# A hybrid encoder layer on one core: seven block products instead of eight for the left half of the second feed-forward matrix in blocks 1 to 3, placed between row blocks of the first matrix

## The chip, the core and the metric

The kernel runs on one core of one Trainium2 chip. Its time is the device time of that core in microseconds (us), from the first to the last instruction. Before the change it is 1097.86 us, the median of 3 runs (1096.95 to 1099.26). Engines are named as in the profile: PE (matmuls), PEld (weight loads of PE), DVE (vector engine), ACT (scalar engine), POOL (GpSimd) and SP (the queue that issues most loads).

## The reference, cut to what matters

One layer: a windowed attention sub-layer, then a feed-forward sub-layer, each with a modulation by the vector c ahead of it and a LayerNorm behind it. The change touches the feed-forward part alone.

```python
D_MODEL, SEQ, D_FF = 2048, 256, 8192
def sq_relu_mlp(h, w1, b1, w2, b2):
    u = jnp.square(jax.nn.relu(h @ w1 + b1))      # (256, 8192)
    return u @ w2 + b2                            # (256, 2048)

mod = c_act @ mod_w[i] + mod_b[i]
sh_m, sc_m, g_m, sh_f, sc_f, g_f = jnp.split(mod, 6, axis=-1)
...
hmlp = x * (1.0 + sc_f) + sh_f
y = sq_relu_mlp(hmlp, mlp_w1[i], mlp_b1[i], mlp_w2[i], mlp_b2[i])
x = layer_norm(DEEPNORM_ALPHA * x + (1.0 + g_f) * y, ln_mlp_g[i], ln_mlp_b[i])
```

All of it is float32.

## The kernel before

A float32 product is made of three matmuls on rounded operands: each operand is split into a high part (a cast) and a low part (the rest), and high by high, high by low and low by high are summed in PSUM. `mm3` (L497 to L500) issues the three; its 128 x 512 output takes three matmuls of 512 columns.

**The weight stream.** `Stream` holds a queue of pieces of weights, each 128 x 2048 in float32 (1 MB), in the order in which the program uses them. `loads` (L196) issues them from SP into the buffers of the pool `raws` (5 in this stage); ACT casts each half of a piece to a `wh` tile of 128 x 1024 (L247), DVE subtracts that from the piece to make the `wl` tile (L218), and there are 5 buffers for either kind. `main` hands the next piece to the matmuls, and `done` says that PE has finished with half a piece. Some pieces are not for matmuls: 16 pieces `in_modgf` make the feed-forward gate, each two DVE instructions of 1024 columns (L345).

**The feed-forward part.** The 8192 hidden units are worked in 4 blocks of 2048. Block 0's first matrix (L971 to L973) is built another way and isn't touched. For blocks 1 to 3 `ff_hidden` makes 16 row blocks of 128 hidden units: 16 times a matmul of 512 columns (L995, weights high; the right side is the input's high and low part side by side, 256 each) and one of 256 columns (L996, weights low) into one PSUM bank. `square_halves` then adds the two halves of the bank (ACT L943, DVE L944), squares what is above zero (DVE L946), and splits it (ACT L948, DVE L949) into `u`, two row blocks to a tile. `ff_out` multiplies all 2048 hidden units of the block by 512 columns of the second matrix, for 4 column groups c and 2 row halves t of the sequence: 96 matmuls of 512 columns for each c. Their result is added to `ys` by DVE; in the last block `add_gated` applies the gate, adds the input and takes the statistics.

So in each block a stage of row blocks (L995, L996) is followed by a stage of output (L498 to L500). A tile scheduler sets the order on each engine from the program's order and the buffers that come free; each engine then runs its own queue strictly in that order. PSUM has 8 banks: pool `psa` with 5 (names pa), `pst` with 2 (pt), `psm` with 1 (pm).

Of the kernel before, what the change touches and what calls it, by code (L numbers as in the profile page):

```python
# [20 lines left out]
S = 256  # L21
# [27 lines left out]
def hybrid_kernel(ctx: ExitStack, tc: tile.TileContext, a, out: bass.AP):  # L49
# [55 lines left out]

    def masks():
        msk = cst.tile([128, NT, 256], F32, name="msk")
# [8 lines left out]
    def rotary_tables():  # L116
# [17 lines left out]
        trig = cst.tile([128, 2, 3, NT, 32], F32, name="trig")  # L134
# [39 lines left out]
    class Stream:  # L174
# [4 lines left out]
        def __init__(self):  # L179
# [11 lines left out]
            self.side = {}  # L191

        def plan(self, src, use=None, kept=0):
            self.q.append((src, use, kept))

# [9 lines left out]
        def freed(self, n):  # L205
            if self.deep or self.home[n] is raws:
                self.free.append(self.home[n])
# [6 lines left out]
        def low(self):  # L214
            n = len(self.ls)
            r, kept = self.src[n]
            l = (g4, g4b)[kept - 1](F32R) if kept else wlp.tile([128, 1024], F32R, name="wl")
            self.pinned(nc.vector.tensor_sub(l, r, f32(self.hs[n])))  # L218
            self.ls.append(l)
            if n % 2:  # L220
                self.freed(self.of[n])

        def pump(self, vecs, must=0):

            while len(self.ls) < must or self.at < len(self.q):
# [17 lines left out]
                if n >= must and (n - self.used >= self.nh or kept):  # L243
                    return
                h = (g4, g4b)[kept - 1](F32R) if kept else whp.tile([128, 1024], F32R, name="wh")
                s = self.raw[self.at][:, n % 2 * 1024:n % 2 * 1024 + 1024]
                self.pinned(nc.scalar.copy(h, s))  # L247
                self.hs.append(h)
                self.src.append((s, kept))
                self.of.append(self.at)  # L250
                self.at += n % 2

        def main(self):
            i = self.im
            self.pump(self.pace, 2 * i + 2)
            self.im += 1
            h, l = self.hs[2 * i:2 * i + 2], self.ls[2 * i:2 * i + 2]
# [219 lines left out]
    for blk in range(BLK):  # L477
        for f in range(NF):
            if blk:
                if blk == 1 and f % 2:  # L480
                    if f == 1:
                        first_gf = len(S.q)
                    m_gf.plan()
                S.plan(a["w1b"][(blk - 1) * NF + f])
        for c in range(4):
            for kg in range(4):
                if blk == 1 and kg % 2:
                    m_gf.plan()
                S.plan(a["w2"][blk, c, kg], None, max(kg - 1, 0) if blk == BLK - 1 and c == 3 else 0)
# [401 lines left out]
    S.stop = 0  # L891
# [48 lines left out]
    def square_halves(ps, ft, u, at):  # L940
# [235 lines left out]
```

## Time and profile before

| what | us |
|---|---|
| median of 3 runs | 1097.86 |
| span of the profiled execution | 1098.2 |
| PE busy | 1067.6 |
| DVE busy | 804.2 |
| ACT busy | 522.0 |
| POOL busy | 30.0 |

The page lists, among other things, busy time for each engine, the chain of work that ended last, and groups of instructions by line with their mean duration. The views drawn on below are the windows (busy time of each engine in a stretch), the timeline (single instructions in order of time), the groups of instructions with shapes kept apart, and the list of transfers. A matmul's duration in these views holds its way through the array and overlaps the next one, so what one costs is the distance between two starts.

### The profile page before, as it was taken

The numbers are of one execution on the slowest core, as the hardware profiler recorded it, in microseconds if no ns is written. First come the engines' busy times: TensorE is split into PE (matmuls) and PEld (weight loads), VectorE is DVE, ScalarE is ACT, GpSimd is POOL, SyncE is SP. The second block draws the span as 40 slices with busy tenths as digits, with TensorE's granted clock in tenths as the row PEclk, the third lists the DMA queues.
The fourth block names the chain that finished last, engine by engine and source line by source line (L and its number), as shares of the span: only waits on it lengthen the run. The fifth ranks groups of instructions, "written<-read, shape, count | busy, mean of one in ns | idle before, by whom it ended". The sixth has DMA issues, their size and how long they took to land.

```text
span 1098.2 us, 15487 instructions
## 1 busy us (share of the span) xinstructions
PE 1067.6 (97%) x6098; PEld 863.1 (79%) x6098; DVE 804.2 (73%) x1162; ACT 522.0 (48%) x806; POOL 30.0 (3%) x54
## 2 busy tenths in 40 slices
PE   8889999998999999999999999999999999999995
PEld 6657677665677799988888888888888888888884
DVE  4597899978899877754588889756666557665676
ACT  5333346765673537643344543344453334544340
POOL 1000000001000000000000010001000000000001
PEclk9989999999999999999999999999999999999998
DMA  9999987789985996555578788866555555557511
GB/s 384 425 427 425 427 357 280 271 297 379 377 315 201 361 360 244 185 192 192 195 301 303 272 313 306 312 220 225 184 189 190 197 196 186 178 185 267 191 75 77
DMA packets 43337, 292.70 MB, mean 267 GB/s; under 512 B 5104, under 2 KB 5232, under 8 KB 9472
## 3 DMA queue, kind: packets, MB, share of 16 engines
q1 hardware_dynamic: 39312, 279.85, 66.9%
q0 software_dynamic: 3200, 10.50, 2.7%
q10 hardware_dynamic: 752, 1.35, 0.3%
q8 instruction: 48, 0.79, 0.3%
q14 instruction: 25, 0.20, 0.0%
HBM read 289.57 MB, written 2.11 MB: 266 GB/s over the span
## 4 chain that ended last, share of the span: by engine, by line
PE 86%; DVE 7%; DMA 4%; ACT 2%; issue 1%; DVEq 0%; ACTq 0%
PE pa L995 16%; PE pa L500 15%; PE pa L498 15%; PE pa L499 15%; PE pa L996 8%; PE pa L972 3%; PE pa L971 3%; PE pa L973 3%; PE pm L307 3%; DVE wl L218 2%; DMA raw<-in_modm 2%; DMA raw<-in_modf 1%; DVE g L345 1%; DMA raw<-in_wqkv 1%; PE pa L687 1%; PE pa L743 1%
## 5 line engine op out<-in xcount | busy, mean ns | idle before, releaser
L218 DVE TENSOR_TENSOR wl<-raw,wh 128x1024 fp32r<-128x1024 f32 x332 | 403.9, 1223 | 223.6 <-ACT wh L247 222.9
L247 ACT CAST wh<-raw 128x1024 fp32r<-128x1024 f32 x332 | 347.1, 1051 | 441.3 <-PE pa L500 228.6
L498 PE MATMUL pa<-wh,g 128*128 128x512 f32 x816 | 324.1, 398 | 5.1 <-ACT g L519 2.6
L500 PE MATMUL pa<-wh,g 128*128 128x512 f32 x816 | 318.9, 392 | 4.1 <-DVE g L521 3.0
L499 PE MATMUL pa<-wl,g 128*128 128x512 f32 x816 | 320.0, 392 | 0.0
L995 PE MATMUL pa<-g,wh 128*128 128x512 f32 x768 | 270.1, 397 | 0.0
L996 PE MATMUL pa<-g,wl 128*128 128x256 f32 x768 | 214.9, 280 | 0.0
L498 PEld LDWEIGHTS pa<-wh,g 128*128 128x128 f32 x816 | 153.9, 189 | 46.8 <-issue 7.5
L500 PEld LDWEIGHTS pa<-wh,g 128*128 128x128 f32 x816 | 153.5, 188 | 41.2 <-DVE g L521 6.0
L499 PEld LDWEIGHTS pa<-wl,g 128*128 128x128 f32 x816 | 153.9, 189 | 33.0 <-issue 2.4
L995 PEld LDWEIGHTS pa<-g,wh 128*128 128x128 f32 x768 | 144.2, 188 | 36.0 <-issue 0.8
L996 PEld LDWEIGHTS pa<-g,wl 128*128 128x128 f32 x768 | 144.8, 189 | 0.1
L345 DVE SCALAR_TENSOR_TENSOR g<-raw,cact,g 128x1024 f32<-128x1024 f32 x65 | 82.6, 1280 | 2.8 <-DMA raw<-in_modf 2.3
L972 PE MATMUL pa<-g,wh 128*128 128x256 f32 x256 | 72.7, 285 | 0.4 <-DVE g L915 0.4
L971 PE MATMUL pa<-g,wh 128*128 128x256 f32 x256 | 72.5, 286 | 0.0
L973 PE MATMUL pa<-g,wl 128*128 128x256 f32 x256 | 72.3, 283 | 0.0
L307 PE MATMUL pm<-raw,cact 128*32 128x256 f32 (+2 forms) x776 | 48.8, 375 | 5.9 <-DMA raw<-in_modf 3.2
L971 PEld LDWEIGHTS pa<-g,wh 128*128 128x128 f32 x256 | 48.8, 192 | 1.3 <-issue 0.8
L972 PEld LDWEIGHTS pa<-g,wh 128*128 128x128 f32 x256 | 49.1, 192 | 0.9 <-DVE g L915 0.8
L973 PEld LDWEIGHTS pa<-g,wl 128*128 128x128 f32 x256 | 49.1, 192 | 0.0
L345 DVE SCALAR_TENSOR_TENSOR g4b<-raw,cact,g4b 128x1024 f32<-128x1024 f32 x32 | 40.7, 1280 | 9.0 <-DMA raw<-in_modgf 8.8
L307 PEld LDWEIGHTS pm<-raw,cact 128*32 128x32 f32 x776 | 20.9, 112 | 25.9 <-issue 11.5
(165 smaller groups left out, 741.6 us busy)
## 6 DMA issues: line engine op xcount, KB each, us to landing
raw<-in_w SPq DMA_DIRECT2D x64, 1024.0 KB, 4.9
raw<-in_w1b SPq DMA_DIRECT2D x48, 1024.0 KB, 5.0
raw<-in_modm SPq DMA_DIRECT2D x32, 1024.0 KB, 14.8
raw<-in_modf SPq DMA_DIRECT2D x32, 1024.0 KB, 6.9
raw<-in_wqkv SPq DMA_DIRECT2D x24, 1024.0 KB, 12.8
raw<-in_modgm SPq DMA_DIRECT2D x16, 1024.0 KB, 7.5
raw<-in_wo SPq DMA_DIRECT2D x16, 1024.0 KB, 7.5
raw<-in_w1a SPq DMA_DIRECT2D x16, 1024.0 KB, 7.6
```

What stands on the lines that cost most here:

```text
L218: self.pinned(nc.vector.tensor_sub(l, r, f32(self.hs[n])))
L247: self.pinned(nc.scalar.copy(h, s))
L307: i = nc.tensor.matmul(self.ps[32 * j:32 * j + 32, :w], lhsT[j] if type(lhsT) is list else lhsT, rhs[j], start=self.first, stop=stop)
L345: nc.vector.scalar_tensor_tensor(p[:, :e], s, cact[:, kt:kt + 1], p[:, :e], op0=OP.mult, op1=OP.add)
L498: nc.tensor.matmul(ps, xh, wh, start=start, stop=False)
L499: nc.tensor.matmul(ps, xh, wl, start=False, stop=False)
L500: S.prev = nc.tensor.matmul(ps, xl, wh, start=False, stop=stop).ins
L971: nc.tensor.matmul(o, wh(w, 128), hh, start=new, stop=False)
L972: nc.tensor.matmul(o, wh(w, 128), hl, start=False, stop=False)
L973: nc.tensor.matmul(o, wl(w, 128), hh, start=False, stop=end)
L995: nc.tensor.matmul(ps, wh(k, 128), hb, start=k == 0, stop=False)
L996: nc.tensor.matmul(ps[:, :256], wl(k, 128), hb[:, :256], start=False, stop=k == NK - 1)
```

## The change

**The products.** Take two row blocks of hidden units (k = 0, 1; a pair), the two sequence halves (t = 0, 1), and the column groups c = 0 and 1. That is a product of a 2 x 2 by a 2 x 2 matrix of blocks, eight block products before. Now there are seven, each over sums and differences of blocks (a Strassen-Winograd form), summed over the 8 pairs of a block in seven PSUM banks `pm[1]` to `pm[7]`. The sums of the hidden values are made by `sides` on DVE (tile `sc`), those of the weights by `sums` on DVE, in place in the loaded piece; at the block's end `gather` adds the seven banks to the four parts of `ys`. The right half (c = 2, 3) goes through `ff_out` as before.

**The order.** `ff_mixed` replaces `ff_hidden`. After row blocks 0 and 1 and 2, each pair i gives the products 1, 2, 3, then row block 2i+3, then the products 5, 7, 6, 4, then row block 2i+4. In a row block 8 matmuls of 512 columns now stand ahead of 8 of 256. With four `psa` banks taken by products, one is left for row blocks.

**The stream.** A piece for the products (`in_w2s`, 24 of them) makes four high and four low tiles (one of 512 columns, three of 1024); the last two pairs of tiles live in buffers of `raws`, of which 2 of the 5 are set aside (`reserve`).

**Moved.** The 16 gate pieces now lie between the pieces of block 0's output (14), and one each in blocks 1 and 2 (before: block 1). The bias b2 is loaded by quarters; the rescaling of the input goes to blocks 1 and 2, the gating of the finished parts (`base`) into block 3's stage. The square is taken on ACT (`square_half`) instead of DVE. Two small constant tables share the buffer of `sc`.

```diff
@@ Stream
+        def sums(self, raw, j):
+            while len(self.ls) < len(self.hs) - 1 and j > 1:
+                self.low()
+            if j == 2:
+                nc.vector.tensor_sub(raw[:, :1024], raw[:, 512:1536], raw[:, :1024])
+            if j == 3:
+                nc.vector.tensor_sub(raw[:, 1024:1536], raw[:, 1024:1536], raw[:, :512])
+                nc.vector.tensor_sub(raw[:, 1536:], raw[:, 1536:], raw[:, 1024:1536])
+            if j < 2:
+                return whp.tile([128, 1024], F32R, name="wh"), raw[:, :512] if j == 0 else raw[:, 1024:], None
+            x = raws.tile([128, 2048], F32R, name="raw")
+            return x[:, :1024], raw[:, 1024 * j - 2048:1024 * j - 1024], x[:, 1024:]
...
+    gf_fill = [1, 1, 1, 1, 1, 1, 1, 1, 1, 1, 1, 1, 1, 1, 0, 0, 1, 0, 0, 0, 0, 0, 0, 0, 1, 0, 0, 0, 0, 0, 0, 0]
...
+    for blk in range(1, BLK):
+        w1 = [a["w1b"][(blk - 1) * NF + f] for f in range(NF)]
+        S.plan(w1[0])
+        S.plan(w1[1])
+        for i in range(NP):
+            if i + 1 < NP:
+                S.plan(w1[2 * i + 2])
+            S.plan(a["w2s"][blk - 1, i], None, -1)
+            if i + 1 < NP:
+                S.plan(w1[2 * i + 3])
+        for c in (2, 3):
+            plan_out(blk, c)
...
-    def square_halves(ps, ft, u, at):
+    def square_half(ps, ft, u, uf, at):
         v = sml.tile([128, 512], F32, name="rl", tag="t2", bufs=4)
         nc.scalar.activation(v[:, 256:], ps[:, 256:], AF.Identity, bias=b1[:, ft:ft + 1])
         nc.vector.tensor_add(v[:, :256], v[:, 256:], ps[:, :256])
-        uf = sml.tile([128, 512], F32, name="uf", tag="t2", bufs=4)[:, :256]
-        nc.vector.scalar_tensor_tensor(uf, v[:, :256], 0.0, v[:, :256], op0=OP.max, op1=OP.mult)
+        nc.scalar.activation(v[:, 256:], v[:, :256], AF.Relu)
+        w = uf[:, at:at + 256]
+        nc.scalar.activation(w, v[:, 256:], AF.Square)
         h, l = u[:, at:at + 256], u[:, 512 + at:512 + at + 256]
-        nc.scalar.copy(h, uf)
-        nc.vector.tensor_sub(l, uf, f32(h))
+        nc.scalar.copy(h, w)
+        nc.vector.tensor_sub(l, w, f32(h))
+    def sides(uf):
...
+        nc.vector.tensor_add(q(0), p(1), p(3))
+        nc.vector.tensor_sub(q(1), q(0), p(0))
+        nc.vector.tensor_sub(q(2), p(0), p(1))
+        nc.vector.tensor_sub(q(3), p(2), q(1))
+        nc.scalar.copy(sc[:, :512], sf)
+        nc.vector.tensor_sub(sc[:, 512:], sf, f32(sc[:, :512]))
+        return sc
...
+            for k0 in (0, 8):
+                for k in range(k0, k0 + 8):
+                    nc.tensor.matmul(ps, wh(k, 128), ff_in(k), start=k == 0, stop=False)
+                for k in range(k0, k0 + 8):
+                    nc.tensor.matmul(ps[:, :256], wl(k, 128), ff_in(k)[:, :256], start=False, stop=k == NK - 1)
+                S.done()
...
+            product(1, i, u, 0, h[0], l[0], 0)
+            S.done()
+            product(2, i, u, 2, h[1], l[1], 1)
+            product(3, i, sc, 3, h[1], l[1], 0)
+            S.done()
+            yield
+            product(5, i, sc, 0, h[2], l[2], 0)
+            product(7, i, sc, 2, h[2], l[2], 1)
+            S.done()
+            product(6, i, sc, 1, h[3], l[3], 0)
+            product(4, i, u, 3, h[3], l[3], 1)
+            S.done()
+        hidden(0)
+        hidden(1)
+        sc = sides(pairs[0])
+        for i in range(NP):
+            g = chunk(i)
+            if i + 1 < NP:
+                hidden(2 * i + 2)
+            next(g)
+            if i + 1 < NP:
+                hidden(2 * i + 3)
+            for _ in g:
+                pass
+            if i + 1 < NP:
+                sc = sides(pairs[i + 1])
+            if i and more:
+                more.pop(0)()
+        return us, pm
+    def gather(pm):
...
+        return [add(y[0], y[0], pm[2]), lambda: nc.scalar.copy(w, pm[6]), add(y[1], y[1], pm[3]),
+                add(y[2], y[2], pm[4]), add(y[0], y[0], pm[1]), add(w, w, pm[1]), add(y[1], y[1], w),
+                add(y[1], y[1], pm[5]), add(y[3], y[3], pm[5]), add(w, w, pm[7]), add(y[2], y[2], w),
+                add(y[3], y[3], w)]
```

The next rows are the queues as built, with what each instruction waits for; lines are those of each version's own code.

PE, in the middle of a block, at the row block that stands between products 3 and 5 of a pair; `pt` and `pa` are PSUM banks, `sc` the tile of hidden sums, `raw` a buffer that holds weight sums. Before, in the row blocks:

```order
L995 MATMUL pa<-g_3389,wh 128x512 [waits Activation_49]
L996 MATMUL pa<-g_3389,wl 128x256 [waits DVE_49]
L995 MATMUL pa<-g_3389,wh 128x512
L996 MATMUL pa<-g_3389,wl 128x256
L995 MATMUL pa<-g_3390,wh 128x512
```

Now:

```order
L545 MATMUL pa<-wl,sc 128x512
L546 MATMUL pa<-wh,sc 128x512 [waits DVE_49]
L544 MATMUL pt<-raw,sc 128x512
L1060 MATMUL pa<-g_3388,wh 128x512 [waits DVE_49]
L1060 MATMUL pa<-g_3388,wh 128x512
L1060 MATMUL pa<-g_3389,wh 128x512 x2
L1060 MATMUL pa<-g_3551,wh 128x512 x2
L1060 MATMUL pa<-g_3552,wh 128x512 x2
L1062 MATMUL pa<-g_3388,wl 128x256 x2
L1062 MATMUL pa<-g_3389,wl 128x256 x2
```

Products now lie between row blocks (in most pairs one matmul of product 5 goes ahead), the two widths stand in groups, and a row block's first matmul waits for DVE: for the add that empties the one bank.

DVE, between the adds that empty that bank after an odd row block (the first L990) and after the next even one (the last). L230 is a low part of weights, L996 a low part of hidden values, L1004 to L1009 the hidden sums. Before, for one row block and the next:

```order
L944 TENSOR_TENSOR rl<-rl,pa 128x256 [waits Activation_49]
L946 SCALAR_TENSOR_TENSOR uf<-rl 128x256 [waits DVE_49]
L218 TENSOR_TENSOR wl<-raw,wh 128x1024 [waits PE_49,Activation_49]
L949 TENSOR_TENSOR g_6904<-uf,g_6904 128x256 [waits Activation_49]
L218 TENSOR_TENSOR wl<-raw,wh 128x1024 [waits DMAHW4_49,PE_49,Activation_49]
```

Now (tile numbers kept, since rows read alike; pa_7286 is the odd row block's bank, pa_7367 the even one's):

```order
L990 TENSOR_TENSOR rl_7329<-rl_7329,pa_7286 128x256 [waits Activation_49]
L230 TENSOR_TENSOR raw_7353<-raw_7258,raw_7353 128x1024 [waits Activation_49]
L230 TENSOR_TENSOR raw_7386<-raw_7258,raw_7386 128x1024 [waits DVE_49,Activation_49]
L996 TENSOR_TENSOR g4_7215<-uf_7216,g4_7215 128x256 [waits Activation_49]
L1004 TENSOR_TENSOR sf_7358<-uf_7216 128x128
L1005 TENSOR_TENSOR sf_7358<-sf_7358,uf_7216 128x128 [waits DVE_49]
L230 TENSOR_TENSOR wl_7432<-raw_7284,wh_7420 128x1024 [waits PE_49,Activation_49]
L1007 TENSOR_TENSOR sf_7358<-uf_7216,sf_7358 128x128 [waits DVE_49]
L1009 TENSOR_TENSOR sc_7357<-sf_7358,sc_7357 128x512 [waits Activation_49]
L230 TENSOR_TENSOR wl_7455<-raw_7327,wh_7430 128x1024 [waits DMAHW1_49,PE_49,Activation_49]
L990 TENSOR_TENSOR rl_7410<-rl_7410,pa_7367 128x256 [waits Activation_49]
```

Where two low parts and three small instructions stood between two such adds, nine stand now, and two of them write into buffers of `raws`.

ACT, at the end of block 1, at the block's last row block (bank pa_6366). L277 is a cast of weights, L991 and L993 the rectifier and the square, L995 the high part of the hidden values:

```order
L989 ACTIVATE rl_6408<-pa_6366,pack_87 128x256 [waits PE_49]
L277 CAST raw_6423<-raw_6257 128x1024 [waits PE_49]
L991 ACTIVATE rl_6408<-rl_6408 128x256 [waits DVE_49]
L993 ACTIVATE uf_6296<-rl_6408 128x256 [waits Activation_49]
L995 CAST g4_6295<-uf_6296 128x256 [waits Activation_49]
L1008 CAST sc_6441<-sf_6442 128x512 [waits DVE_49,PE_49]
```

A cast into a buffer that PE must release now stands between the first step of the last row block's square and the rest of it; the products of the last pair, which need that square, have no row block ahead of them.

More of the change, by code (lines that the diff above doesn't have):

```diff
@@ L982, in hybrid_kernel, with ff_mixed, hidden @@
                 us.append(u)
-    def ff_hidden(blk):
-        nonlocal g2
-        us = []
-        for f in range(NF):
+    def ff_mixed(blk, more=()):
+        more = list(more)
+        us, sc, pairs = [], None, []
+        pm = {}
+        def hidden(f):
             ft = blk * NF + f
@@ L999, in ff_hidden @@
[L999 to L1002 removed]
+            for k0 in (0, 8):
[4 more added lines that the diff above has]
+                S.done()
+            square_half(ps, ft, us[-1], pairs[-1], (f % 2) * 256)
@@ L1044, in hybrid_kernel @@
-        S.stop = 0
+            if blk:
+                rescale(2 * blk + c - 4)
+        if blk == 0:
+            S.reserve = 2
     blk = BLK - 1
-    us = ff_hidden(blk)
+    g2 = gate(m_gf)
+    us, pm = ff_mixed(blk, [lambda c=c, t=t: base(c, (t,)) for c in (2, 3) for t in range(NT)])
     gb = [[g4(), g4()], [g4(), g4()]]
```

179 lines of the change are left out of this document (111 added, 68 removed).

## The prediction

> **What bounds the kernel now.** I read the page's head and its chain of waits first, then busy time by stage, then single instructions for distances. The chain that ended last runs through PE for most of the span:
>
> ```profile
> span 1098.2 us, 15487 instructions
> PE 86%; DVE 7%; DMA 4%; ACT 2%; issue 1%; DVEq 0%; ACTq 0%
> ```
>
> The windows of the feed-forward part show busy time of each engine in a stage. The seven stages are the output of block 0, then row blocks and output of blocks 1, 2 and 3:
>
> ```profile
> core 0: us, PE busy (x) PEld busy (x) DVE busy (x) ACT busy (x) POOL busy (x), PEclk, DMA share, GB/s
> 466.40:553.40 87.00, 87.00 (x386) 72.05 (x385) 48.39 (x47) 35.49 (x36) 0.95 (x1) 1.00 0.54 193
> 553.40:643.90 90.50, 90.50 (x514) 78.49 (x514) 76.55 (x97) 44.07 (x62) 1.50 (x2) 1.00 0.79 295
> 643.90:731.00 87.10, 87.10 (x387) 72.11 (x386) 66.42 (x70) 34.40 (x34) 3.76 (x7) 1.00 0.80 298
> 731.00:821.10 90.10, 90.10 (x522) 77.84 (x520) 56.62 (x79) 44.42 (x63) 3.05 (x6) 1.00 0.56 199
> 821.10:908.20 87.10, 87.10 (x387) 72.13 (x386) 51.09 (x54) 34.33 (x34) 0.00 (x0) 1.00 0.55 193
> 908.20:998.60 90.40, 90.40 (x513) 78.35 (x512) 58.86 (x83) 43.75 (x62) 2.11 (x4) 1.00 0.55 191
> 998.60:1085.70 87.10, 87.10 (x386) 71.92 (x384) 53.94 (x65) 30.65 (x32) 1.75 (x1) 1.00 0.42 152
> ```
>
> PE has no gap in 619 us and runs at full clock. DVE is at 56 to 85%, ACT near half. So a matmul taken out is worth its whole distance, as long as DVE and ACT, which get more work, still deliver in time. What a matmul costs is the distance of starts. Three in the output stage, two in a row block, the gate's own eight in block 2, three of 256 columns in block 0's first matrix:
>
> ```profile
> 1084.31 0.39 PE L498 MATMUL pa<-g4b,g 128*128 128x512 f32 x1
> 1084.99 0.39 PE L498 MATMUL pa<-g4b,g 128*128 128x512 f32 x1
> ...
> 590.18 0.40 PE L995 MATMUL pa<-g,wh 128*128 128x512 f32 x1
> 590.42 0.28 PE L996 MATMUL pa<-g,wl 128*128 128x256 f32 x1
> 590.54 0.40 PE L995 MATMUL pa<-g,wh 128*128 128x512 f32 x1
> ...
> 742.34 1.06 PE L307 MATMUL pm<-g4b,onesf 128*32 128x512 f32 x8
> 743.34 0.50 PE L995 MATMUL pa<-g,wh 128*128 128x512 f32 x1
> ...
> 430.03 0.28 PE L971 MATMUL pa<-g,wh 128*128 128x256 f32 x1
> 430.39 0.28 PE L971 MATMUL pa<-g,wh 128*128 128x256 f32 x1
> ```
>
> That is 0.227 us for 512 columns (87.1 us for the stage's 384 says the same), 0.353 for a mixed two (90.5 for 256 of them), 0.12 for 256 columns among their like.
>
> **The change, part by part.**
>
> *Products.* Of eight, one goes: 3 blocks x 8 pairs x 3 matmuls = 72 x 0.227 = **-16.3 us**.
>
> *Widths in groups.* A row block of 16 mixed twos takes 16 x 0.353 = 5.65; in groups, from the other two distances, 16 x (0.227 + 0.12) = 5.55. For 256 twos that is 88.8 against 90.5 in blocks 1 and 3, and against 89.1 in block 2 (90.1 less 1.0 for the gate's own matmuls): -1.7, -0.4, -1.7 = **-3.8**. The other end is 0, if the order of widths doesn't matter.
> The Trainium skill (TensorE: Matmul & The Clock Gate, "Back-to-back issue gap") gives a gap by a matmul's own columns, N / 2.4 ns + 2.5 ns. By it a mixed two would be 325 ns in either order, and this term 0; the rows show 353, so the page's law doesn't hold for mixed widths here, and the term stays.
>
> *Work given to DVE and ACT.* Durations and, where two stand back to back, distances:
>
> ```profile
> L218 DVE TENSOR_TENSOR wl<-raw,wh 128x1024 fp32r<-128x1024 f32 x332 | 403.9, 1223 | 223.6 <-ACT wh L247 222.9
> L946 DVE SCALAR_TENSOR_TENSOR uf<-rl 128x256 f32<-128x256 f32 x48 | 20.4, 424 | 1.4
> 1045.46 2.35 DVE L218 TENSOR_TENSOR wl<-raw,wh 128x1024 fp32r<-128x1024 f32 x2
> 1063.62 1.28 DVE L751 TENSOR_TENSOR tmp<-pa,g4b 128x512 f32<-128x512 f32 x2
> 604.14 2.48 DVE L345 SCALAR_TENSOR_TENSOR g4b<-raw,cact,g4b 128x1024 f32<-128x1024 f32 x2
> 592.49 0.42 DVE L949 TENSOR_TENSOR g<-uf,g 128x256 fp32r<-128x256 f32 x1
> 592.83 1.28 DVE L345 SCALAR_TENSOR_TENSOR g4b<-raw,cact,g4b 128x1024 f32<-128x1024 f32 x1
> 590.26 1.05 ACT L247 CAST wh<-raw 128x1024 fp32r<-128x1024 f32 x1 [1.36 <-PE pa L995]
> 591.22 0.40 ACT L948 CAST g<-uf 128x256 fp32r<-128x256 f32 x1
> ```
>
> So DVE needs 1.14 for 1024 columns (2.35 - 1.22), 0.60 for 512, 0.34 for 256; L345 1.20; ACT 0.96 for 1024. For 128 columns no row stands; between 0 and 0.34, I take 0.2. A pair now costs DVE eight of 1024 (seven low parts, one sum), four of 512, four of 256, four of 128: 9.1 + 2.4 + 1.4 + 0.8 = 13.7 us. PE needs 2 x 5.55 + 21 x 0.227 = 15.9 for it. ACT needs 7 x 0.96 + 2 x 0.5 + 8 x 0.43 = 11.2. Nothing exceeds PE by the sum, but DVE goes to 86%, and its queue is strict, so I walked it.
>
> *The one bank.* Before, a row block's bank was emptied while the next filled another. Now the next row block waits for ACT L989 and DVE L990 and is covered by products alone: 12 matmuls (2.72) after an odd row block, 9 or 10 (2.04 or 2.27) after an even one. A result is there 0.39 after its matmul's start, as the last one shows, so 0.17 after the next could start; L943 and L944 are now L989 and L990, and bare of queues the emptying takes 0.17 + 0.47 + 0.42 = 1.1:
>
> ```profile
> 1085.45 0.39 PE L500 MATMUL pa<-g4b,g 128*128 128x512 f32 x1
> 1085.87 0.69 DVE L751 TENSOR_TENSOR tmp<-pa,g4b 128x512 f32<-128x512 f32 x1 [2.13 <-PE pa L500]
> ...
> L943 ACT ACTIVATE rl<-pa,pack 128x256 f32<-128x256 f32 x48 | 22.4, 466 | 0.0
> L944 DVE TENSOR_TENSOR rl<-rl,pa 128x256 f32<-128x256 f32 x48 | 19.9, 415 | 0.6 <-ACT rl L943 0.5
> ```
>
> The walk, in us from the end of an odd row block: product 7 ends at 1.36 and frees a buffer for the first weight sum; its cast on ACT runs 1.6 to 2.6, its low part on DVE to 3.9. The second sum's cast waits for product 4 (2.9 to 4.0), its low part ends at 5.2. Square and split of the hidden values follow (L991, L993, L995 to 4.8; L996 to 5.5), two hidden sums to 6.0, a low part to 7.2, L1007, its cast and L1009 to 8.7, a low part to 10.2, and L990 for the even row block, which ended at 2.72 + 5.55 = 8.27, is done at 10.5. The next row block could start at 10.3 or, with one matmul of product 5 ahead, 10.5: a wait of 0 to 0.2. From there on DVE has 6.9 us of work to the next L990, which is done at 17.8, before it is needed (18.8). So the loop closes with PE in the lead by a hair. I take 0.1 for each of 21 pairs: **+2**; from below 0, from above 0.6 (half a low part standing wrong) x 21 = 13.
> The Trainium skill (Perfetto Trace Analysis, "Optimizing Tensor Performance") asks that independent groups of matmuls rotate through different PSUM banks, so that emptying one overlaps the next; for row blocks the change gives that up. If its warning decided, the time would be that of rival 5; no run here shows one bank yet.
>
> *The ends of the blocks.* The last pair has no row block ahead. After the last row block PE has four products (2.72), then product 1 needs that block's square. On ACT the cast for the second weight sum stands ahead of L991 and waits for product 4: 2.9 to 4.0, then L991, L993, L995 to 5.1 (block 3, with one more cast between them, 6.0). PE stands **2.4, 2.4 and 3.3 = +8**. With nothing ahead of L991 the chain would end at 2.5 and cost 0, the lower end; the upper is 3 x 4. Behind product 1 PE has matmuls of the output ready, so the hidden sums, about 2.5 later, don't stop it again.
>
> *Moves.* Block 0's output gets 14 gate pieces: DVE 32 x 1.14 + 28 x 1.20 + 8 x 0.6 = 75 of 87 us. Its loads are 30 x 1.05 MB in 87 us, 361 GB/s, where this program has moved up to 427:
>
> ```profile
> GB/s 384 425 427 425 427 357 280 271 297 379 377 315 201 361 360 244 185 192 192 195 301 303 272 313 306 312 220 225 184 189 190 197 196 186 178 185 267 191 75 77
> raw<-in_w1b SPq DMA_DIRECT2D x48, 1024.0 KB, 5.0
> raw<-in_modgf SPq DMA_DIRECT2D x16, 1024.0 KB, 6.7
> ```
>
> PE covers both; with 5 buffers I add **+1** (0 to 4). Blocks 1 and 2 lose 32 DVE instructions less four. In block 3 four gatings of 1.2 us fall into the pairs' loop, which has no room: 4 x 0.5 = **+2** (0 to 4.8). `gather`, 11 adds of 0.6 a block, lies in the output stage, where DVE has 21.8 us for 8 x 1.14 + 6.6 + 3.6 = 19.4; nothing. The last matmul to the end (12.5 us) stays.
>
> Sum: -16.3 - 3.8 + 2 + 8 + 1 + 2 = -7.1, from the profiled span 1098.2 to 1091.1. The span is 0.3 over the median of the runs, so **1091 us**.
>
> **The rivals.**
>
> 1. *The waits are hidden.* The block ends and loops cost 4 instead of 13: PE's products cover the bank, and the squares come sooner than my queue has them. For it: the scheduler put fillers at each place. Against: the cast ahead of L991 is in the queue. 1098.2 - 20.1 + 4 = 1082.
> 2. *Slower: late loads.* Two of five load buffers are gone. In the walk the product piece's load starts when its forerunner's last low part ends (5.2) and is needed at 10.2: 5.0 us, just the `in_w1b` landing time. At the 6.7 of `in_modgf` its cast comes 1.8 late, and on ACT it stands ahead of L991; 0.9 of that is slack before the next L990. 21 x 0.9 = 19: 1110. It decides from 0.43 per pair (9 us to the old time). For it: three buffers, one at a time. Against: loads run at some 200 GB/s there, where 5.0 was seen; 6.7 came at 295.
> 3. *The clock falls at the block ends.* In the first 40 us the granted clock dips once:
>
> ```profile
> 20.00:30.00 10.00, 6.93 (x84) 5.07 (x84) 4.86 (x6) 7.26 (x11) 0.00 (x0) 1.00 1.02 426
> 30.00:40.00 10.00, 8.73 (x84) 6.34 (x85) 3.18 (x7) 2.85 (x4) 0.00 (x0) 0.83 1.01 424
> ```
>
>    3.1 us idle out of 10 left it at 1.00, yet the next 10 ran at 0.83, 1.7 us lost. Three times that is +5: 1096. [...]
> 4. *The widths' order is worth nothing.* Block 2's row blocks came at 0.348 for a mixed two (89.1 / 256) against 0.353, so the distance isn't fixed by the order alone. Then 1091 + 3.8 = 1095. That is what the Trainium skill's gap law, named above, would give.
> 5. *The one bank covers nothing*: 42 row blocks wait out the whole emptying, 42 x 1.1 = 46, less the 2 in the sum: 1135. For it: each row block's first matmul does wait for DVE in the queue. Against: 9 to 12 matmuls stand between, twice the bare 1.1.
>
> **How the numbers follow.** This kernel's runs can tell about 0.2%, 2.2 us, from no change. The forecast, 1087 to 1096, has 0.49; rival 1 0.17; rival 2 0.16; rival 3 0.08; rival 4 0.07; rival 5 0.03. Faster (under 1095.7): 0.49 + 0.17 and half of rival 4, 0.03, less 0.02 for the forecast's upper edge: 0.67. Same: that 0.02, rival 3's 0.08 and the other 0.04: 0.14. Slower: rivals 2 and 5, 0.19. The range runs from rival 1 at 1082 (0.07 lies below it) to 1103 (0.13 above it), where the four added terms, 2, 8, 1 and 2, reach three quarters of their upper ends (13 + 12 + 4 + 4.8 = 34).
>
> **What would show it.** Matmuls 0.227 apart in the products and 0.12 in the groups of 256: the first two terms. Idle time ahead of L1060, put down to DVE L990, of some 2 us in all in blocks 1 to 3 confirms the loop; over 10 refutes it. Idle time of PE three times, of 2 to 3.5 us, released by ACT L995 ahead of a product into `pt`: the block ends. ACT waiting for `in_w2s` would be rival 2, a granted clock under 1.00 behind the ends rival 3. If DVE's busy share passes 95% in the pairs, my durations are wrong.

## The result, and the profile after

| | before | after |
|---|---|---|
| median of the runs, us | 1097.40 (4 runs, 1095.14 to 1099.26) | 1083.86 (4 runs, 1082.19 to 1085.78) |
| span of the profiled execution, us | 1098.2 | 1084.0 |
| from the first row block of block 1 to the last matmul, us | 532.0 | 519.4 |

The ratio is 0.989, with a 95% interval of 0.9874 to 0.9905: faster by 13.5 us, 1.1%. The forecast was 1091, faster by 7.

The head of the page of after, its busy times and its chain of waits:

```profile
span 1084.0 us, 15688 instructions
PE 1051.5 (97%) x6026; PEld 846.6 (78%) x6026; DVE 926.1 (85%) x1371; ACT 611.3 (56%) x977; POOL 31.0 (3%) x56
PE 81%; DVE 9%; DMA 7%; ACT 2%; issue 1%; SPq 0%; DVEq 0%; ACTq 0%
```

PE has 72 matmuls less (6098 before), DVE 122 us more, ACT 89 us more, and PE still carries the chain. The windows of after by stage, columns as in the prediction: output of block 0, then mixed stage and right half of blocks 1, 2 and 3:

```profile
464.80:551.90 87.10, 87.10 (x387) 72.11 (x386) 72.33 (x68) 35.91 (x36) 2.17 (x4) 1.00 0.89 350
551.90:676.50 124.60, 124.60 (x664) 106.35 (x662) 111.81 (x156) 87.31 (x132) 0.00 (x0) 1.00 0.47 169
676.50:721.50 45.00, 45.00 (x199) 36.87 (x198) 36.01 (x45) 19.55 (x21) 2.15 (x4) 1.00 0.82 315
721.50:848.50 127.00, 126.95 (x672) 107.97 (x671) 112.21 (x156) 87.66 (x131) 0.00 (x0) 1.00 0.47 170
848.50:893.50 45.00, 45.00 (x199) 36.85 (x198) 36.03 (x47) 20.20 (x23) 2.15 (x4) 1.00 0.81 307
893.50:1021.00 127.50, 127.50 (x679) 107.81 (x678) 114.73 (x162) 88.20 (x132) 5.14 (x10) 1.00 0.52 188
1021.00:1071.50 50.50, 50.24 (x221) 40.73 (x219) 45.63 (x68) 17.64 (x22) 1.75 (x1) 1.00 0.42 166
```

Block 0's output takes 87.1 us as before, with DVE at 72.3 us and 350 GB/s: the gate pieces cost nothing there. In the mixed stages DVE is at 90%, ACT at 70%, the granted clock at 1.00 throughout. PE looks full, but a busy PE can hide short waits, so the next view is the one of the add that empties the bank, DVE L990, and shows for how long the row blocks' weight loads waited for it (us, times):

```profile
  PEld pa L1060: 4.5, 12
```

The timeline shows such a wait (start, duration, engine, line; idle time and its releaser in brackets):

```profile
601.36 0.46 ACT L989 ACTIVATE rl<-pa,pack 128x256 f32<-128x256 f32 x1
...
601.49 1.23 DVE L230 TENSOR_TENSOR wl<-raw,wh 128x1024 fp32r<-128x1024 f32 x1 [0.26 <-ACT wh L277]
...
602.63 0.41 DVE L990 TENSOR_TENSOR rl<-rl,pa 128x256 f32<-128x256 f32 x1
602.76 0.39 PE L544 MATMUL pt<-raw,sc 128*128 128x512 f32 x1
...
603.10 2.12 PE L1060 MATMUL pa<-g,wh 128*128 128x512 f32 x8
```

ACT was done with the bank at 601.82; DVE had a low part of weights in front, so L990 came 0.8 us later, and the row block started 0.34 after the matmul before it instead of 0.23. The second distance behind the wait is 0.34 too (the group of eight takes 2.12; where nothing waits, 2.00). So a wait costs PE some 0.22 us (0.11 in each of the two distances; the 4.5 us of the view are the weight loads', which start ahead of their matmuls). By the starts of the matmuls the 12 waits in blocks 1 to 3 cost 2.7 us.

The end of block 1, the products of the last pair (PE from the last row block's end at 673.07, then ACT):

```profile
673.07 0.40 PE L544 MATMUL pt<-raw,sc 128*128 128x512 f32 x1
...
675.82 0.39 PE L544 MATMUL pt<-wh,g 128*128 128x512 f32 x1
...
676.50 0.39 PE L544 MATMUL pa<-wh,g 128*128 128x512 f32 x1
...
676.95 0.39 PE L546 MATMUL pa<-wh,g 128*128 128x512 f32 x1
677.31 0.50 PE L544 MATMUL pa<-wh,g 128*128 128x512 f32 x1
```

```profile
674.66 1.05 ACT L277 CAST raw<-raw 128x1024 fp32r<-128x1024 f32 x1
675.95 0.42 ACT L991 ACTIVATE rl<-rl 128x256 f32<-128x256 f32 x1 [0.23 <-DVE rl L990]
676.40 0.42 ACT L993 ACTIVATE uf<-rl 128x256 f32<-128x256 f32 x1
676.85 0.41 ACT L995 CAST g<-uf 128x256 fp32r<-128x256 f32 x1
```

No stall of 2.4 us. Product 1 (into `pt`) runs at 675.82, before the last row block's square exists; three matmuls of the output follow (676.50 to 676.95), and product 2, which does need the square, starts at 677.31, 0.13 late. The cast at 674.66 starts before product 4's last matmul (675.59), so it did not wait for product 4; and L991 behind it waited for DVE's add L990 (0.23), not for the cast.

### The profile page after: what moved, and what is told of

It reads as the page before. It is cut to its first block, busy times and chain, and to the rows that moved or that the text cites. A ratio compares the mean times of both kernels' runs of the same rounds, so it can differ in the third digit from the quotient of the medians.

```text
span 1084.0 us, 15688 instructions
## 1 busy us (share of the span) xinstructions
PE 1051.5 (97%) x6026; PEld 846.6 (78%) x6026; DVE 926.1 (85%) x1371; ACT 611.3 (56%) x977; POOL 31.0 (3%) x56
## 3 DMA queue, kind: packets, MB, share of 16 engines
q10 hardware_dynamic: 752, 1.35, 0.3%
## 4 chain that ended last, share of the span: by engine, by line
PE 81%; DVE 9%; DMA 7%; ACT 2%; issue 1%; SPq 0%; DVEq 0%; ACTq 0%
PE pa L1060 17%; PE pa L544 12%; PE pa L546 12%; PE pa L545 12%; PE pa L1062 8%; DMA raw<-in_modm 4%; PE pa L1033 3%; PE pa L1032 3%; PE pa L1034 3%; DVE wl L230 3%; PE pm L340 2%; DVE g L378 2%; DMA raw<-in_wqkv 1%; DMA raw<-in_modf 1%; PE pa L733 1%
## 5 line engine op out<-in xcount | busy, mean ns | idle before, releaser
L277 ACT CAST wh<-raw 128x1024 fp32r<-128x1024 f32 (+1 forms) x332 | 335.5, 1020 | 288.8 <-PE pa L546 143.6
L230 DVE TENSOR_TENSOR wl<-raw,wh 128x1024 fp32r<-128x1024 f32 (+1 forms) x332 | 387.8, 1181 | 77.0 <-ACT wh L277 71.5
L544 PE MATMUL pa<-wh,g 128*128 128x512 f32 x648 | 258.4, 399 | 5.2 <-ACT g L565 2.1
L546 PE MATMUL pa<-wh,g 128*128 128x512 f32 x648 | 252.8, 393 | 3.7 <-DVE g L567 3.0
L545 PE MATMUL pa<-wl,g 128*128 128x512 f32 x648 | 254.5, 393 | 0.3 <-DVE wl L230 0.3
L1060 PE MATMUL pa<-g,wh 128*128 128x512 f32 x768 | 193.5, 393 | 0.0
L544 PEld LDWEIGHTS pa<-wh,g 128*128 128x128 f32 x648 | 121.9, 188 | 41.2 <-issue 7.8
L546 PEld LDWEIGHTS pa<-wh,g 128*128 128x128 f32 x648 | 121.8, 188 | 34.5 <-DVE g L567 6.0
L1062 PEld LDWEIGHTS pa<-g,wl 128*128 128x128 f32 x768 | 104.7, 190 | 7.6
L1062 PE MATMUL pa<-g,wl 128*128 128x256 f32 x768 | 107.0, 282 | 0.0
L1034 PE MATMUL pa<-g,wl 128*128 128x256 f32 x256 | 72.3, 283 | 0.0
L230 DVE TENSOR_TENSOR raw<-raw 128x1024 fp32r<-128x1024 f32 x48 | 58.5, 1221 | 8.6 <-ACT raw L277 7.0
L277 ACT CAST raw<-raw 128x1024 fp32r<-128x1024 f32 x48 | 50.6, 1054 | 13.2 <-PE pm L546 9.8
L1034 PEld LDWEIGHTS pa<-g,wl 128*128 128x128 f32 x256 | 49.1, 192 | 0.0
```

The lines of the kernel that those rows point to most:

```text
L230: self.pinned(nc.vector.tensor_sub(l[:, :w], r, f32(self.hs[n])[:, :w]))
L277: self.pinned(nc.scalar.copy(h[:, :s.shape[-1]], s))
L544: nc.tensor.matmul(ps, xh, wh, start=start, stop=False)
L545: nc.tensor.matmul(ps, xh, wl, start=False, stop=False)
L546: S.prev = nc.tensor.matmul(ps, xl, wh, start=False, stop=stop).ins
L1034: nc.tensor.matmul(o, wl(w, 128), hh, start=False, stop=end)
```

## The experiments

Where a kernel's lines moved by one to four, its own numbers stand in the rows. "The stage" is from the first row block of block 1 to the last matmul; it came out within 0.1 us in two profiles of the changed kernel, while its start lies anywhere between 548.5 and 553.5 us over 14 profiles (the kernel before 553.5, the changed one 551.9 and 550.8). So stages are compared to a tenth, total times by their intervals.

### What the seven products, the interleaving and the widths are worth

**eight**: the seven products are eight again, in the same places.

```diff
-            product(1, i, u, 0, h[0], l[0], 0)
...
+            for k in range(2):
+                for j in range(2):
+                    for t in range(NT):
+                        x, p = (2 * k + t) * 128, 2 * k + j
+                        mm3(pm[2 * t + (j ^ k)], u[:, x:x + 128], u[:, 512 + x:640 + x], wh(p), wl(p),
+                            i == 0 and k == 0, i == NP - 1 and k == 1)
```

> Left half of blocks 1 to 3 as eight plain products into four banks, at the same places between the row blocks; no sums of weights or hidden values, all five load buffers free. Count theory (the gain is the 72 matmuls): they come back, 72 x 0.227 = +16.3 on 1083.9; the waits for the one bank (14 times some 0.23 = 3.3 us in the changed kernel) go, since four banks are left for row blocks and DVE has less to do: 1097. Rival (the interleaving, the widths in groups and the moved gate pieces made most of the gain, and seven products give back in waits what they save): 1084 to 1090.

Measured: 1095.5 us, ratio 0.999 (0.9972 to 1.0007). The stage (length, then busy times of PE, PEld, DVE, ACT):

```profile
548.80:1079.20 530.40, 530.40 (x2697) 452.18 (x2696) 315.35 (x368) 271.35 (x383) 11.21 (x19) 1.00 0.56 195
```

519.4 to 530.3, +10.9: the 16.3 us of the 72 matmuls come back, and some 5.4 us of waits and of slower matmuls behind them go (PE never waits for the bank's add). The rival falls: with eight products, the interleaving and the moved gate pieces are worth nothing beyond the widths in groups, since the next kernel, which has those alone, has the same stage.

**grouped**: the kernel before, with the changed kernel's loop over the two widths, and **alternating**: the changed kernel with the old loop.

```diff
-            for k in range(NK):
-                nc.tensor.matmul(ps, wh(k, 128), hb, start=k == 0, stop=False)
-                nc.tensor.matmul(ps[:, :256], wl(k, 128), hb[:, :256], start=False, stop=k == NK - 1)
+            for k0 in (0, 8):
+                for k in range(k0, k0 + 8):
+                    nc.tensor.matmul(ps, wh(k, 128), ff_in(k), start=k == 0, stop=False)
+                for k in range(k0, k0 + 8):
+                    nc.tensor.matmul(ps[:, :256], wl(k, 128), ff_in(k)[:, :256], start=False, stop=k == NK - 1)
```

> The kernel before with the two widths of a row block in groups of eight, nothing else. By the traces' distances -2.5 on 1097.4: 1094.9. The prediction's term -3.8: 1093.6. A gap by a matmul's own columns: 1097.4.

> The changed kernel with the two widths of a row block alternating again, nothing else. From the traces, a 512 and a 256 cost 351.4 ns together before and 348.2 ns in groups, without the waits: 768 x 3.2 ns = +2.5, so 1086.4. The prediction's term: +3.8, so 1087.7. A gap that depends on a matmul's own columns alone: no change, 1083.9.

Measured: grouped 1095.5 us, ratio 0.9987 (0.9971 to 1.0003), alternating 1091.54 us, 0.9946 (0.9924 to 0.9967). The stages, grouped first:

```profile
552.70:1083.10 530.40, 530.40 (x2697) 452.28 (x2696) 363.30 (x446) 233.58 (x287) 12.16 (x20) 1.00 0.62 222
```

```profile
551.00:1078.10 527.10, 522.48 (x2625) 434.52 (x2623) 455.46 (x629) 315.77 (x458) 11.23 (x19) 1.00 0.53 195
```

Alone, the grouping takes 1.7 us off (532.0 to 530.3). In the changed kernel its loss costs 7.7 (519.4 to 527.1), twice what any theory had, and it is not a matter of distances alone: more than half of it is PE standing idle (527.1 less 522.5 busy is 4.6; 0.3 in the changed kernel), 2.7 for the cast of the hidden sums and 1.6 for the bank's add. What fits, but was not tried apart: with the widths alternating, the low weights are needed from the row block's first matmuls on, in groups 1.8 us later, and DVE at 90% lives on that slack.

### One bank

**side_by_side**: the program calls both row blocks of a pair and then all seven products.

```diff
-            next(g)
             if i + 1 < NP:
                 hidden(2 * i + 3)
+            next(g)
```

> The changed kernel with the two row blocks of a pair next to each other and the seven products behind both, so that the second row block has no cover for the one bank. Cover theory: the second row block waits for the whole emptying, 1.1 us bare and up to 2.3 with DVE's queue, 21 times, less the 3.3 us of waits of the changed kernel that go: +20 to +45, so 1104 to 1129, with idle time ahead of the row block's matmuls put down to DVE's add. Rival (the scheduler finds other work, or the bank is no matter): within 3 us of 1083.9.

Measured: 1084.37 us, ratio 0.9885 (0.9859 to 0.9912), the stage 519.5 us. The scheduler took the products ahead of the second row block again, as soon as they were ready; but for the first pair of a block, the trace has the changed kernel's alternation on PE. The experiment tested nothing, and was made again with PE's order fixed:

**side_by_side_forced**:

```diff
+                    if behind: tc.add_manual_dep(m, behind, ORDER_ONLY, reason="side")
...
+            if last: tc.add_manual_dep(m[0], last, ORDER_ONLY, reason="side")
...
+                hidden(2 * i + 2, i and S.prev.name)
+                last = hidden(2 * i + 3)
```

> As side_by_side, but with PE's order fixed: in each pair both row blocks stand next to each other and all seven products behind them. Cover theory: the second row block waits 1.05 (0.16 for the last result, 0.47, 0.41) and 0.1 for the first weights, with DVE's queue up to 2.4, 21 times: +22 to +47 after the 3.4 of the loop's waits are taken off, 1106 to 1131, with distances of 1.3 to 2.6 us ahead of a row block 21 times. Rival (the add and the activation overlap with something, the bank is no matter): under 1090.

Measured: 1136.77 us, ratio 1.0363 (1.0344 to 1.0383), the stage 571.8, +52.4. Who waited for the add (here L991), a wait on the timeline, and the windows around it (last three columns: granted clock, DMA share, GB/s):

```profile
  PE pa L1061: 37.1, 18
```

```profile
621.89 3.50 PE L1061 MATMUL pa<-g,wh 128*128 128x512 f32 x8 [2.28 <-DVE rl L991]
```

```profile
615.00:620.00 5.00, 4.61 (x28) 3.92 (x26) 3.97 (x5) 3.69 (x5) 0.00 (x0) 1.00 0.28 120
620.00:625.00 5.00, 3.11 (x8) 2.51 (x9) 3.40 (x5) 2.41 (x5) 0.00 (x0) 0.72 0.13 31
625.00:630.00 5.00, 5.00 (x29) 4.44 (x29) 1.94 (x3) 2.48 (x3) 0.00 (x0) 0.93 0.64 220
```

Without cover the starts on either side of the wait stand 1.8 to 2.6 us apart, 18 times (the first pair of a block still finds free banks), 42 us in all where 18 x 0.12 = 2 would stand without a wait. Some 12 more come from the clock, which the expectation did not have: behind each of the nine longest waits the granted clock fell, 39 matmuls of 512 columns stood 0.427 us apart (0.2 lost with each) and some 50 of 256 columns 0.214 (0.09 each). So it is the cover of 9 to 12 product matmuls that makes one bank nearly free, and the scheduler keeps that cover by itself.

### The ends of the blocks

**end_in_order**: in the last pair product 2 goes ahead of product 1, and the output behind both.

```diff
-            product(1, i, u, 0, h[0], l[0], 0)
-            S.done()
-            product(2, i, u, 2, h[1], l[1], 1)
+            if i < NP - 1:
+                product(1, i, u, 0, h[0], l[0], 0)
+                S.done()
+            two = product(2, i, u, 2, h[1], l[1], 1)
+            if i == NP - 1:
+                one = product(1, i, u, 0, h[0], l[0], 0)
+                tc.add_manual_dep(one[0], two[1].name, ORDER_ONLY, reason="2 first")
+                S.tail = one[1].name
+                S.done()
```

> The changed kernel with, in each block's last pair, product 2 (which needs the last row block's square) ahead of product 1, and the output's matmuls behind both: the order of work that the prediction's walk of the block ends assumed. The walk: PE stands 2.4, 2.4 and 3.3 us, +8 on 1083.9: 1092. By the changed kernel's trace the square's high part was there 1.5 us after product 4's last matmul, so 1.5 to 1.7 an end plus some 0.1 each for the first weights behind the wait, less the 0.6 that the three ends cost now: +4.5, 1088. If the ends cost nothing in either order: 1084.

Measured: 1088.69 us, ratio 0.9925 (0.9906 to 0.9944), the stage 524.4, +5.0. The end of block 1, from product 4's last matmul to product 2's first:

```profile
674.59 0.39 PE L547 MATMUL pa<-raw,g 128*128 128x512 f32 x1
676.30 0.50 PE L545 MATMUL pa<-wh,g 128*128 128x512 f32 x1 [1.33 <-ACT g L997]
```

The starts around the wait are 1.72, 1.71 and 1.89 apart at the three ends, 1.5 to 1.7 late. The walk's 2.4 to 3.3 is too much even in its own order of work: ACT's cast for the second weight sum ran at 673.65 there, ahead of product 4's first matmul (674.13), so it had not waited for it. The other 5 of the 8 us are missing in the changed kernel because product 1 and the output go ahead.

### Taking the loop's waits away

**bank_first**: low parts asked for between two row blocks stand behind the bank's add on DVE.

```diff
-            self.pinned(nc.vector.tensor_sub(l[:, :w], r, f32(self.hs[n])[:, :w]))
+            i = nc.vector.tensor_sub(l[:, :w], r, f32(self.hs[n])[:, :w])
+            if self.bank: tc.add_manual_dep(i.ins, self.bank, ORDER_ONLY, reason="bank first")
```

> The changed kernel with the low parts of weights that are asked for between a row block and the next put behind the add that empties the bank, in DVE's queue; no work added or removed. Queue theory (a low part that stands ahead of the add makes the 14 waits): most of their 3.3 us go, 1081. Rival (DVE has no room in the pairs, so what is put behind comes late for a product): 1084 or more, with waits for low parts or for the hidden sums in place of those for the bank.

Measured: 1085.16 us, ratio 0.9894 (0.9876 to 0.9912), the stage 519.5. The edit also drops an order that held low parts in the attention part, ahead of the stage, so here and in the next three kernels the stage is what to compare. All waits for the bank are gone, so a low part in the queue made them. But in blocks 1 and 2 the end now stalls:

```profile
672.35 0.39 PE L545 MATMUL pa<-wh,g 128*128 128x512 f32 x1
674.86 0.50 PE L545 MATMUL pa<-wh,g 128*128 128x512 f32 x1 [2.12 <-ACT g L996]
```

```profile
669.12 0.48 ACT L990 ACTIVATE rl<-pa,pack 128x256 f32<-128x256 f32 x1 [4.68 <-PE pa L1063]
669.99 1.06 ACT L278 CAST wh<-raw 128x1024 fp32r<-128x1024 f32 x1 [0.39 <-DMA raw<-in_w]
670.95 1.05 ACT L278 CAST raw<-raw 128x1024 fp32r<-128x1024 f32 x1
671.90 0.41 ACT L992 ACTIVATE rl<-rl 128x256 f32<-128x256 f32 x1
672.21 1.03 ACT L278 CAST raw<-raw 128x1024 fp32r<-128x1024 f32 x1
673.15 0.41 ACT L994 ACTIVATE uf<-rl 128x256 f32<-128x256 f32 x1
673.47 1.03 ACT L278 CAST wh<-raw 128x1024 fp32r<-128x1024 f32 x1
674.40 0.40 ACT L996 CAST g<-uf 128x256 fp32r<-128x256 f32 x1
```

Four casts of weights stand among the steps of the last square: the stall that the prediction described (casts ahead of the square on ACT), in a kernel whose queue has them there, though here they hold the square by their own length and not by a wait for product 4.

**bank_and_square_first** frees the last row block of the rule and puts the casts asked for behind its square; **best_wide_groups** adds groups of 16.

```diff
+            if f < NF - 1: S.act = None
+            else: S.bank = None
...
+                if self.act: tc.add_manual_dep(i.ins, self.act, ORDER_ONLY, reason="square first")
```

> bank_first, but in each block's last row block no low part is put behind the add, and the casts of weights asked for after it stand behind that block's square on ACT. If the two parts are separate costs (bank 14 x 0.23 = 3.3, the ends as bank_first showed them): the bank's waits stay away, the ends fall from 2.3 and 2.0 to under 0.5 each: the feed-forward part of blocks 1 to 3 at 515 to 516 us instead of 519.4, the time 3 to 4 under that of the changed kernel run beside it. If DVE's lack of room only moves the stall about, as in bank_first: no difference.

> The kernel above with a row block as 16 matmuls of 512 columns and then 16 of 256. In the changed kernel the first five matmuls of 512 behind a group of 256 stand 228 to 236 ns apart instead of 227, 27 ns in all for each of 96 groups; half of the groups less is 48 x 0.027 = 1.3 us off. Rival (tiles of weights are held for longer and the low parts come late): 1 us or more on top, with waits for DMA or for casts.

Measured: 1088.57 us, ratio 0.992 (0.9898 to 0.9943), stage 521.2; and 1086.84 us, 0.9902 (0.9881 to 0.9923), stage 521.9. Both are worse than the changed kernel: the square came in time, but the weights behind it were late, and single matmuls stood up to 1.4 us from the one before, waiting for a low part. The wide groups brought their 1.2 us (the excess of the matmuls of 512 over 0.227, without the waits, falls from 2.2 to 1.0 us). Their stage is longer all the same, but not through the groups: the waits at the ends are the same in both kernels, and this profile alone lost 1.6 us to the clock, behind a wait at the end of block 2 (last columns of the window: granted clock, DMA share, GB/s):

```profile
848.82 0.76 PE L548 MATMUL pa<-wl,g 128*128 128x512 f32 x1 [1.01 <-DVE wl L230]
```

```profile
848.80:852.30 3.50, 3.48 (x8) 2.78 (x9) 3.50 (x5) 2.52 (x3) 1.07 (x2) 0.51 1.03 339
```

So these two runs leave open what groups of 16 are worth in the total.

**bank_first_to_12**: bank_first for row blocks 0 to 12 of a block only.

```diff
+            x = square_half(ps, ft, us[-1], pairs[-1], (f % 2) * 256)
+            S.bank = x if f <= 12 else None
```

> bank_first for the first 13 of a block's 16 row blocks alone; at the block's end the queues stand close to the changed kernel's, with six or seven matmuls of the output ahead of product 2. If the loop's waits and the end's are separate costs: none of the 14 waits for the bank, ends under 0.5 each, the feed-forward part of blocks 1 to 3 at 516 us (519.4 less 3.3), the time some 3 under 1084. If DVE and ACT have no room for it at all: the ends grow by what the loop gains, as in the two kernels before this, 519 to 521.

Measured: 1080.11 us, ratio 0.9858 (0.9837 to 0.988). The stage:

```profile
549.10:1064.90 515.80, 515.34 (x2625) 437.79 (x2624) 449.05 (x629) 319.81 (x458) 11.22 (x19) 1.00 0.54 199
```

3.7 us less than the changed kernel: no row block waits for the bank, and the ends cost 1.4 in all. Its stage is shorter than that of both kernels, and its total than that of the kernel before; against the changed kernel the intervals of the total overlap (0.9874 to 0.9905, and the next run).

**changed_again**:

> The changed kernel once more, beside the two above on the same chip: 1084, feed-forward part of blocks 1 to 3 at 519.4 us; the start of that part may differ by some us, as it did between the profiles so far (548.8 to 553.5).

Measured: 1083.29 us, ratio 0.9874 (0.9849 to 0.99), the stage 519.3, starting at 550.8.

**sums_on_pool**: the hidden sums on POOL.

```diff
-        nc.vector.tensor_add(q(0), p(1), p(3))
+        nc.gpsimd.tensor_add(q(0), p(1), p(3))
```

> The changed kernel with the four 128-column hidden sums of each pair on POOL instead of DVE; 1.15 us per pair less for DVE (4 x 0.29). If DVE's load makes the waits for the bank, they fall from 14 to a few: -2 to -3, 1081 to 1082. If the chain of the hidden sums (through ACT and back) sets them, and POOL makes that chain longer: 1084 to 1090, with waits for the hidden sums ahead of the products that use them.

Measured: 1104.41 us, ratio 1.0067 (1.0048 to 1.0086), the stage 539.6. Two of the four adds, and a DVE instruction of the loop with its least, median and greatest duration (its mean is 419 ns in the changed kernel):

```profile
L1004 POOL TENSOR_TENSOR sf<-uf 128x128 f32<-128x128 f32 x24 | 28.7, 1197 | 179.1 <-ACT uf L993 179.1
L1007 POOL TENSOR_TENSOR sf<-uf,sf 128x128 f32<-128x128 f32 x24 | 26.6, 1108 | 1.9
```

```profile
L996 DVE TENSOR_TENSOR g<-uf,g x48: 407/678/692, 562.4 to 1045.7; 128x256 fp32r<-128x256 f32 x48
```

The second theory held in kind, with another place and far past its 1090: the sums' chain became longer (means of 0.6 to 1.2 us an add, 0.285 on DVE), DVE waited 24.6 us for the cast of the sums (9.6 in the changed kernel), and the bank's add stood behind it, so PE waited for the bank, 0.4 to 1.6 us each time. Less work on DVE did not help; what stands ahead of the add did harm. Some 1.4 us are again the clock's (seven matmuls 0.427 apart from 863.93 on, behind a wait of 2.1 idle).

## Why the prediction was right in sign and half in size

In us, measured by the starts of matmuls in the stage:

| term | predicted | measured |
|---|---|---|
| products, 72 x 0.227 | -16.3 | -16.3 |
| widths in groups | -3.8 | -1.7 (grouped) |
| the one bank in the loop | +2 | +2.7 |
| ends of the blocks | +8 | +0.7 |
| gate pieces into block 0 | +1 | 0.0 (87.07 both) |
| gatings in block 3's loop | +2 | +0.3 at most |
| not in the sum: the first pair's product 3 late for its sums 0.53, a low part late in the last output 0.53, matmuls of 512 a little slower 0.81 | 0 | +1.9 |
| the sum | -7.1 | -12.4 by terms, -12.6 read from the stage |
| ahead of the stage | 0 | -1.5 |

The -1.5 lies ahead of the stage. The two kernels built from the old one start it at 553.5 and 552.8, the twelve others between 548.6 and 552.6; but eight and grouped, one of either kind and with equal stages, both have a median of 1095.5. So no gain ahead of the stage is shown.

That the total came out within a factor of two is in part luck: the ends were 7.3 too dear and the gatings 1.7, while the widths were 2.1 too hopeful and 1.9 us of other waits were in no term.

**The failed step is the ends of the blocks**: "After the last row block PE has four products (2.72), then product 1 needs that block's square." Product 1 takes columns 0 to 127 of `u`, which are of the even row block and were written long before. The first product that needs the odd one is 2, three matmuls later, and the scheduler put output matmuls ahead of it. That "the cast for the second weight sum stands ahead of L991 and waits for product 4" was half wrong: it stands there, but it ran before product 4 was done. The high part of the square was there 4.2 us after the last row block (677.26 less 673.07), not 5.1. What remains is 0.7 instead of 8. end_in_order puts the order that was assumed onto the chip and gets +5; bank_first has the cast queue that was assumed and gets 2.3 and 2.0 us at two ends. So a late square does stop PE where nothing else stands ahead of its reader; in the changed kernel's queue something does.

**The one bank**: mechanism and place were right. The walk had the wait after an even row block alone, where 9 or 10 matmuls cover, 0 to 0.2 us each; 11 of the 12 waits are there. The size was partly luck: 0.1 for each of 21 pairs was forecast, and half as many waits cost 0.22 each, because a wait is paid a second time in the distance behind it, which the walk did not have.

**Widths**: the sign was right, the size half. The distances 0.227 and 0.12 hold inside a group, but behind each group of 256 the first five matmuls of 512 take 0.233, 0.236, 0.228, 0.233 and 0.231 (mean over 96 groups). Nor is the alternating distance one number: grouping took 1.1 us off in blocks 1 and 3 each, and added 0.4 in block 2, where two of the kernel before take 0.348 together instead of 0.353. The Trainium skill (TensorE: Matmul & The Clock Gate, "Back-to-back issue gap") has, for an isolated matmul, a gap by its own columns, by which the order would not matter; between the kernel before and grouped, where PE waits for nothing but the gate, the two orders differ by 1.7 us, so the trace does not agree.

**Gatings**: block 3 has three waits for the bank, block 1 four and block 2 five, so the gatings added none. One late low part of the sums (at 965.54) is block 3's own; it comes 13 us behind the last gating in the loop, so it isn't shown to be theirs.

**The rivals.** 1, the waits are hidden, at 1082, is close to what happened, and its fillers and its sooner square are both in the trace; what it lacks is that the product that needs the square is a later one. 2, late loads, did not come:

```profile
raw<-in_w2s SPq DMA_DIRECT2D x24, 1024.0 KB, 4.7
...
ACT wh L277 <- DMA raw<-in_w2s: 1.7, 3, 0.9
```

The product pieces landed in 4.7 us, as bounded by the nearest row, and ACT waited for three of 24. (From the forecast to the old time it is 7 us, not the 9 of rival 2's paragraph, so 0.34 a pair would have decided.) 3, the clock, had no stall to follow: 1.00 throughout; one such fall cost 1.6 us in best_wide_groups. 4 falls with grouped, where the order is worth 1.7 us, though its remark that the order alone doesn't fix the distance is borne out by block 2. 5 needed the cover gone; that kernel took 1136.8 us, near rival 5's 1135 by chance, with 18 waits of 2.2 us and the clock in place of 42 of 1.1. The Trainium skill's rule of rotating banks (Perfetto Trace Analysis, "Optimizing Tensor Performance") is borne out where one row block follows the other, at 2.2 us a time; going without it costs 0.22 or nothing where nine or more matmuls of 512 lie between.

The slower matmuls of 512 (0.81 us) are the tail of the waits: the seven that follow a wait's two long distances stand 231 ns apart in the mean (148 of them, 0.66 us in all). The 1177 others of the loop that stand clear of the groups of 256 are at 226.8, and at 226.7 in eight, which has no such waits.

Open: whether three load buffers would be too few at a slower landing, which was not tried.

## What to carry to other kernels

Before a stall at a stage's end goes into the sum, write down for each instruction behind the late result which columns of which tile it reads, and what else a scheduler may put ahead; the sum here failed on one column offset. With DVE at 90%, the order in its queue mattered here and less load did not help: name the one instruction that others wait for (here the add that empties the bank) and keep long independent work behind it. The scheduler undid an order that was only written in the program, so an experiment on order has to fix it on the engine.

## What the runs showed of the hardware that was not expected

- A wait costs PE a second time: behind nearly every one in these traces the first matmul stands 335 to 341 ns ahead of the next instead of 227, some 0.11 us; and the next seven still stand 228 to 235 apart in the mean.
- The clock falls after shorter gaps than thought, and the gap's length alone does not decide. In side_by_side_forced all nine waits with starts 2.56 to 2.63 us apart (2.28 idle in the row above) were followed by matmuls 0.427 apart, the nine of 1.77 to 2.36 by none; the single one of 2.51 in bank_first was not, and one of two of 2.48 in sums_on_pool was. In best_wide_groups it fell behind a distance of 1.40 (1.01 idle, with two more of 0.61 in the 3 us ahead of it), and not behind the same three at the end of block 1. In the kernel before it fell at 30.60, in a gap of 1.35 idle, with two of 1.89 and 0.54 in the 7 us ahead of it. The Trainium skill (TensorE: Matmul & The Clock Gate, "Why this matters for your kernels") names gaps over some 3 us; here less was enough. What decides between them is not shown.
- With the hidden sums on POOL, DVE's L996 took 0.68 us in the median instead of 0.42, and the trace ties this to POOL's adds: the 6 of 48 that ran beside none took 0.41 to 0.42, the 13 with 0.3 us of overlap 0.58 to 0.60, and the 25 with 0.4 to 0.6 us 0.68 to 0.69. Only two that lay wholly beside an add took 0.41.
